# A hybrid RWKV and attention layer on one core: side work in steps of one weight unit, with TensorE's order kept in the chain

## The chip, the cores and the metric

The kernel runs on one core of a Trainium2 chip. The metric is the device time of one execution in microseconds (us), the median of three runs.

## What is computed

One layer of a streaming encoder over 16 meta tokens and 512 frames, width 1024, f32: a half-step feed-forward network (FFN1), the mixing (RWKV-7 heads beside sliding-window attention), a second half-step (FFN2) and a norm. Cut to what matters here:

```python
h = concat([meta, x])                                  # 528 x 1024
h = h + 0.5 * swiglu(rmsnorm(h, ffn1_norm), ...)       # 1024 -> 2816 -> 1024
z = rmsnorm(h, mix_norm) @ w_in
def step(S, inp):                                      # RWKV-7, one token after the other
    r_t, w_t, k_t, v_t, kk_t, a_t = inp
    sa = einsum('bhvk,bhk->bhv', S, -kk_t)
    S = S * w_t[:, :, None, :] + sa[..., None] * (kk_t * a_t)[:, :, None, :] + v_t[..., None] * k_t[:, :, None, :]
    return S, einsum('bhvk,bhk->bhv', S, r_t)
y_rwkv = group_norm_and_gate(scan(step, S0, ...))      # 8 heads of 64
y_attn = swa_sink_attention(q, k, v, sinks)            # chunks of 64, window 128, 8 heads on 2 kv heads
h = h + concat([y_rwkv, y_attn]) @ w_out
h = h + 0.5 * swiglu(rmsnorm(h, ffn2_norm), ...)
return rmsnorm(h, final_norm)[:, 16:]
```

## The kernel before

**The stream.** Activations lie transposed, features on partitions and time on columns, in two halves: the first has 272 columns (16 meta, 256 frames), the second 256. Weights pass as *units* of 128 x 1024: SP loads `raw` from DRAM, ScalarE (ACT) rounds it into `whi` (L122), VectorE (DVE) takes the rest into `wlo` (L125), and TensorE (PE) does 24 matmuls, 16 with `whi` (L213, L214) and 8 with `wlo` (L195, L222), into a bank `big`. `drive` (L128) runs the list of units in the order that `program` writes out. Three units are prepared ahead. A half's attention and RWKV run beside units of the other half or another stage: those of the first half beside FFN1 of the second, those of the second half beside FFN2 of the first. Both must be done before `w_out` of the half, which reads `n0a`/`n0b` (`n1a`/`n1b`). The function `end` (join) stands there.

**The work beside it.** After each unit `advance` (L165) adds the unit's cost to a balance and runs steps of two generators, `rwkv` and `attn`, as long as the balance lasts. A `yield` gives the cost of a step.
- `tinv` (L703): inverts the 32 x 32 triangular diagonal blocks of `GT`, 80 of them, one on each partition. Four DMAs bring the blocks through DRAM into `zk`, then 31 steps on DVE: a product of k x k elements (L726, `tmp`), its sum (L728, into `rn`). Behind the last step come a transposing copy (L731, T1), then writes to DRAM (`d<-rn` L734, `d<-tmp` L735) and reads back into `GT`, `zk`, `t2c`, all from ACT's queue. Two sets of 32 small matmuls (L753 with `zk`, L761 with `t2c`) fill the off-diagonal blocks.
- `chain` (L767): goes through the half's chunks (five in the first, four in the second half) in turn, since state `S` passes from one to the next. `values(n)` (L784) makes a chunk's `UV` and `BT`; then come UV·GT and AR·S (L813, L816), `Rs` (L819, L820), Rs·GT (L828), and the products for `S` and `Y` (L838 to L848). Its banks are `mx`, two of them. `group_norm` (L866) ends each chunk in three steps.
- `attention` (L884): four chunks of 64, each in two pairs of heads: scores (L910), maxima (L916 to L920), exp (L924), scale (L929), transposes (L930, L932), values (L942, L945). It uses the tile `as`, two banks wide, of which there is one.

**What sets the order.** The program is traced in the order above, but each engine's final list is made by a scheduler: it simulates the engines and puts behind one another what is ready in its simulation, by the priorities of `PRIO`. PE works its list strictly in that final order. An instruction that is traced early can so be put later than stream matmuls traced after it, unless its order is pinned.

Of the kernel before, what the change touches and what calls it, by code (L numbers as in the profile page):

```python
# [9 lines left out]
AF = mybir.ActivationFunctionType  # L10
# [24 lines left out]
WARM = 12  # L35
TIW, CHW, ATW = 1.4, 0.55, 0.9
NK = D // 128
# [29 lines left out]


class Prog:
    def __init__(self, ctx, tc, io):  # L70
        self.tc, self.nc, self.io = tc, tc.nc, io
        self.A, self.V, self.P, self.PE = tc.nc.scalar, tc.nc.vector, tc.nc.gpsimd, tc.nc.tensor
        self.uid = 0
        pool = lambda name, **k: ctx.enter_context(tc.tile_pool(name=name, bufs=1, **k))
        self.cst = pool("cst")
        self.rp = pool("res")
        self.np_ = pool("npl")
        self.wp = pool("wpl")
        self.tp = pool("tpl")
        self.sl = [pool("slab0")]  # L80
        self.big = pool("big", space=PSUM)
        self.mx = pool("mx", space=PSUM)
        self.dr = pool("drm", space=DRAM)
        self.hs, self.acc, self.res = {}, {}, {}
        self.sides = []
        self.ph = ''
        self.late = []
# [78 lines left out]
    def advance(self, cost):  # L166
        for sd in list(self.sides):
            if sd not in self.sides:
                continue
            sd[1] += cost  # L170
            while sd[1] > 0:
                self.mark(self.ph or sd[2] if sd[2] == 'rwkv' else sd[2])
                with self.tc.high_priority(PRIO.get(self.ph if sd[2] == "rwkv" else "", PRIO[sd[2]])):
                    c = next(sd[0], None)
                if c is None:
                    self.sides.remove(sd)
                    break
                sd[1] -= c
# [525 lines left out]
    def tinv(self, hf, mp, tip):  # L704
# [42 lines left out]
        self.ph = 'tizo'  # L747
        yield 6.0
        pc = [(p, c, slice((p * 4 + c - 1) * 32, (p * 4 + c) * 32)) for p in range(4) for c in range(1, 5)]
# [5 lines left out]
        for h in range(2):  # L755
            (A.copy, V.tensor_copy)[h](out=Z[hr[h]], in_=bz[hr[h]])
        yield 2.0
        bo = self.mbank()
# [3 lines left out]
        for h in range(2):  # L762
            (A.copy, V.tensor_copy)[h](out=GT[hr[h], 4 * h:4 * h + 4, 1:5, 32:64],
                                       in_=bo[hr[h]].rearrange("p (h s t) -> p h s t", h=4, s=4))
        yield 2.0

    def chain(self, hf, st, mo, cp):  # L767
# [5 lines left out]
        def step():  # L773

            for n_ in list(norms):
                if next(n_, None) is None:
                    norms.remove(n_)
# [4 lines left out]
        def values(n):  # L782


            slot, tok, C = chunks[n]
            UV, BT = t(cp, [128, 2, 4, 64], "UV", bufs=2), t(cp, [128, 2, 4, 64], "BT", bufs=2)
            vr = (slice(64, 64 + C), slice(0, C))
            bs = [self.mbank() for h in range(2)]
            for p in range(4):
                for h, b in enumerate(bs):  # L790
                    PE.matmul(b[vr[h], cols(p)], st["vT", p][hs[h], tok:tok + C], self.cent[hs[h], hs[h]],  # L791
                              start=True, stop=True)
            for p in range(4):
                for r in range(2):
                    for h, b in enumerate(bs):
                        PE.matmul(b[hs[r], cols(p, 256)], self.BK[p][hs[h], slot, hs[r ^ h]], self.ident[hs[h], hs[h]],  # L796
                                  start=True, stop=True)
            for h, b in enumerate(bs):
                A.copy(out=UV[vr[h], h], in_=b[vr[h], 0:256].rearrange("p (j c) -> p j c", j=4))
                A.copy(out=BT[:, h], in_=b[:, 256:512].rearrange("p (j c) -> p j c", j=4))  # L800
            pre[n] = (UV, BT)

        values(0)
        yield CHW
        hp = [(p, h) for p in range(4) for h in range(2)]
        for n, (slot, tok, C) in enumerate(chunks):
# [5 lines left out]
            for p, h in hp:  # L812
                PE.matmul(X[ur[h], cols(p)], gt(vr, h, p, 0), UV[vr[h], h, p], start=True, stop=True)  # L813
            if slot:
                for p, h in hp:
                    PE.matmul(Z[hs[h], cols(p)], self.AR[p][hs[h], slot, 0:64], S[hs[h], p], start=True, stop=True)  # L816
# [7 lines left out]
            step()  # L824
            yield 2 * CHW
            X = self.mbank()
            for p, h in hp:
                PE.matmul(X[ur[h], cols(p)], gt(ur, h, p, 0), Rs[ur[h], cols(p)], start=True, stop=True)  # L828
            for h in range(2):
                (A.copy, V.tensor_copy)[h](out=UV[ur[h], h], in_=X[ur[h], 0:256].rearrange("p (j c) -> p j c", j=4))  # L830
            step()
            yield CHW
            if n + 1 < len(chunks):
                values(n + 1)
            yield CHW
            X, Z = self.mbank(), self.mbank()
# [16 lines left out]
            if slot:  # L853
# [3 lines left out]
                norms.append(self.group_norm(st, mo, cp, Y, slice(64 * slot - 64, 64 * slot)))  # L857
            step()
            yield 2 * CHW
        self.ph = 'gn'  # L860
        while norms:
            step()
            yield 2.0

# [20 lines left out]
    def attention(self, hf, st, mo, ap_):  # L885
        A, V, P, PE, t = self.A, self.V, self.P, self.PE, self.t
        for ci in range(4):
# [16 lines left out]
            A.copy(out=VK[0:81, 0], in_=b[0:81, 0:128])  # L904
            yield ATW
            kss = (slice(0, 64), slice(64, 128))
            for mp2 in range(2):
# [4 lines left out]
                for kv in range(2):  # L912
# [8 lines left out]
                    rows.append((s, m))  # L921
                yield ATW
                for s, m in rows:
                    A.activation(s[:, 0:W], s[:, 0:W], AF.Exp, bias=m[:, 2:3], accum_out=m[:, 3:4])  # L924
                yield ATW
                b, bo = self.banks()
                for kv, (s, m) in enumerate(rows):
                    V.reciprocal(m[:, 3:4], m[:, 3:4])
                    A.activation(s[:, 0:W], s[:, 0:W], AF.Copy, scale=m[:, 3:4])  # L929
                    PE.transpose(b[0:81, 256 * kv:256 * kv + 128], s[:, 0:81], self.ident)  # L930
                    if nw > 1:
                        PE.transpose(b[0:W - 81, 256 * kv + 128:256 * kv + 256], s[:, 81:W], self.ident)  # L932
                yield ATW
                pTs = []
# [8 lines left out]
                if nw > 1:  # L943
                    for kv, ks in enumerate(kss):
                        PE.matmul(bo[ks, 0:128], VK[0:W - 81, 1, ks], pTs[kv][0:W - 81, 1], start=False, stop=True)  # L945
                yield ATW
                ms, ts = slice(2 * mp2, 2 * mp2 + 2), slice(64 * ci, 64 * ci + 64)
# [3 lines left out]
                V.tensor_tensor(out=ml, in0=ov, in1=mh.bitcast(F32), op=ALU.subtract)  # L951
                yield ATW


def program(tc, io, out):
    with ExitStack() as ctx:
# [32 lines left out]
        def popen(name, like=None):  # L989
            c = tc.tile_pool(name=name, bufs=1)  # L990
            pools[name] = (c, c.__enter__())
            return pools[name][1]
# [17 lines left out]
        def mixing(hf):  # L1010
# [8 lines left out]
            def rwkv():  # L1019
                yield from pr.tinv(hf, pools["mix"][1], popen("ti"))  # L1020
                pclose("ti")
                cp = popen("ch")
                yield from pr.chain(hf, st, mo, cp)
                pclose("ch")

            def begin():
# [45 lines left out]
        k = 10  # L1072
# [131 lines left out]
```

## Time and profile before

| | |
|---|---|
| median of 3 runs | 1154.0 us (1153.95 to 1160.99) |
| the profiled execution | 1158.89 us |
| its span on the core | 1156.7 us |
| TensorE's mean granted clock | 0.971 |
| PE busy | 1114.7 us, 96% |
| DVE busy, ACT busy | 826.4 us (71%), 673.0 us (58%) |

In the profile, L12 is line 12 of the kernel; "idle before" is the time in which the engine did nothing ahead of an instruction, and the name behind the arrow is what ended it. A PE row's duration holds the depth of the array; its pitch is the distance of the starts. The granted clock 1.00 is 2.4 GHz. The trace's times count from the start of the span.

### The profile page before, as it was taken

Reading aid. Unit: us, or ns where it says so; the run is one execution under the profiler, and the core shown is the slowest. Engines: PE = TensorE matmul, PEld = TensorE weight load, DVE = VectorE, ACT = ScalarE, POOL = GpSimd, SP = SyncE. Lnnn points to the kernel's source line nnn. Section 1 sums busy time; section 2 is a strip of 40 time slices with the busy share of each in tenths; the row PEclk is TensorE's granted clock in tenths of the full one; section 3 lists DMA queues with packets and bytes.
Section 4 is the critical chain, followed back from the end, with each engine's and each line's share of the span. In section 5 each row is a group of like instructions: output and inputs, shape, how many; then the busy total and the mean of one; then the engine's idle time right before and its main releaser. Section 6 shows DMA issues by size and latency. Waiting matters only on the chain.

```text
span 1156.7 us, 23838 instructions
## 1 busy us (share of the span) xinstructions
PE 1114.7 (96%) x9621; PEld 1043.9 (90%) x9621; DVE 826.4 (71%) x1533; ACT 673.0 (58%) x1162; POOL 36.4 (3%) x91
## 2 busy tenths in 40 slices
PE   8999999999999998999899999997999899999996
PEld 7999999998999997899899898997889898888885
DVE  7866566776778993356888777995356677777666
ACT  7544444686757645565567685574456366545453
POOL 0000000021000000000002000000000000000000
PEclk8999999999999998899899999998899899999999
DMA  7565655544446554223355445556224356676661
GB/s 270 172 182 185 187 177 179 166 142 151 129 137 182 163 176 131 81 93 112 92 182 167 138 134 169 165 152 163 90 76 122 111 154 216 201 205 194 186 186 66
DMA packets 68721, 178.81 MB, mean 155 GB/s; under 512 B 21620, under 2 KB 26868, under 8 KB 68612
## 3 DMA queue, kind: packets, MB, share of 16 engines
q1 hardware_dynamic: 52384, 173.70, 49.1%
q10 hardware_dynamic: 16228, 3.61, 1.5%
q8 instruction: 75, 1.23, 0.4%
q14 instruction: 34, 0.28, 0.1%
HBM read 173.54 MB, written 3.74 MB: 153 GB/s over the span
## 4 chain that ended last, share of the span: by engine, by line
PE 76%; DVE 13%; DMA 4%; ACT 4%; issue 3%; ACTq 1%; SPq 0%; DVEq 0%
PE big L214 16%; PE big L213 16%; PE big L195 12%; PE big L201 10%; PE big L203 5%; DVE wlo L125 4%; PE big L222 4%; DVE tmp L726 3%; DVE rn L728 2%; PE mx L796 1%; ACT whi L122 1%; PE mx L791 1%; DMA d<-GT 1%; DMA res<-xT_in 1%; DMA d<-rn 1%
## 5 line engine op out<-in xcount | busy, mean ns | idle before, releaser
L122 ACT CAST whi<-raw 128x1024 fp32r<-128x1024 f32 (+1 forms) x321 | 334.8, 1045 | 279.0 <-PE big L214 146.8
L125 DVE TENSOR_TENSOR wlo<-raw,whi 128x1024 fp32r<-128x1024 f32 x320 | 389.7, 1219 | 119.0 <-ACT whi L122 96.2
L214 PE MATMUL big<-h,whi 128*128 128x256 f32 (+1 forms) x528 | 135.2, 289 | 0.0
L213 PE MATMUL big<-h,whi 128*128 128x256 f32 (+1 forms) x528 | 132.0, 288 | 0.0
L213 PE MATMUL big<-n0a,whi 128*128 128x272 f32 (+1 forms) x464 | 123.8, 296 | 8.2 <-ACT n0a L881 3.2
L214 PE MATMUL big<-n0a,whi 128*128 128x272 f32 (+1 forms) x464 | 123.1, 293 | 0.6 <-DVE n0a L342 0.6
L213 PE MATMUL big<-n0b,whi 128*128 128x272 f32 (+1 forms) x464 | 120.3, 290 | 0.4 <-ACT n0b L341 0.3
L214 PE MATMUL big<-n0b,whi 128*128 128x272 f32 (+1 forms) x464 | 119.7, 288 | 0.4 <-DVE n0b L342 0.4
L214 PEld LDWEIGHTS big<-h,whi 128*128 128x128 f32 x528 | 100.6, 191 | 1.5 <-issue 0.9
L213 PEld LDWEIGHTS big<-h,whi 128*128 128x128 f32 x528 | 99.7, 191 | 0.6 <-issue 0.3
L213 PEld LDWEIGHTS big<-n0a,whi 128*128 128x128 f32 x464 | 89.6, 194 | 10.6 <-ACT n0a L881 3.4
L214 PEld LDWEIGHTS big<-n0a,whi 128*128 128x128 f32 x464 | 90.0, 194 | 2.1 <-DVE n0a L342 1.0
L213 PEld LDWEIGHTS big<-n0b,whi 128*128 128x128 f32 x464 | 87.9, 190 | 2.0 <-ACT n0b L341 1.1
L214 PEld LDWEIGHTS big<-n0b,whi 128*128 128x128 f32 x464 | 87.8, 190 | 1.6 <-DVE n0b L342 0.7
L213 PE MATMUL big<-n1a,whi 128*128 128x256 f32 x288 | 76.9, 297 | 8.3 <-ACT n1a L881 4.2
L222 PE MATMUL big<-h,wlo 128*128 128x256 f32 (+1 forms) x528 | 81.3, 289 | 0.0
L195 PE MATMUL big<-n0b,wlo 128*128 128x272 f32 (+1 forms) x464 | 77.4, 288 | 0.0
L195 PE MATMUL big<-n0a,wlo 128*128 128x272 f32 (+1 forms) x464 | 76.4, 286 | 0.0
L214 PE MATMUL big<-n1a,whi 128*128 128x256 f32 x288 | 76.2, 293 | 0.0
L214 PE MATMUL big<-n1b,whi 128*128 128x256 f32 x288 | 76.1, 294 | 0.0
L213 PE MATMUL big<-n1b,whi 128*128 128x256 f32 x288 | 75.7, 292 | 0.0
L222 PEld LDWEIGHTS big<-h,wlo 128*128 128x128 f32 x528 | 71.5, 192 | 1.1 <-issue 0.6
(313 smaller groups left out, 2264.2 us busy)
## 6 DMA issues: line engine op xcount, KB each, us to landing
raw<-w_in SPq DMA_DIRECT2D x319, 512.0 KB, 3.8
outT<-o SPq DMA_DIRECT2D x8, 256.0 KB, 2.6
res<-xT_in SPq DMA_DIRECT2D x2, 544.0 KB, 4.3
res<-xT_in SPq DMA_DIRECT2D x2, 512.0 KB, 9.1
d<-GT ACTq DMA_DIRECT2D x8, 80.0 KB, 3.6
zk<-d ACTq DMA_DIRECT2D x2, 320.0 KB, 4.0
d<-rn ACTq DMA_DIRECT2D x2, 320.0 KB, 3.7
GT<-d ACTq DMA_DIRECT2D x8, 80.0 KB, 4.5
```

The source lines that it names most:

```text
L122: self.A.copy(out=hi[:, a:a + n], in_=raw[:, a:a + n])
L125: self.V.tensor_tensor(out=lo[:, 0:nk], in0=raw[:, 0:nk], in1=hi[:, 0:nk].bitcast(F32), op=ALU.subtract)
L195: self.PE.matmul(o, lo[:, k], x(k)[:, 0], start=False, stop=(k == ks[-1]))
L201: self.PE.matmul(o, hi[:, i], x(k).rearrange("p a t -> p (a t)"), start=(k == first), stop=False)
L203: self.PE.matmul(o[:, 0:256], lo[:, i], x(k)[:, 0], start=False, stop=(k == last))
L213: self.PE.matmul(o, w, x[:, 0], start=first, stop=False)
L214: self.PE.matmul(o, w, x[:, 1], start=False, stop=False)
L222: self.PE.matmul(o, lo[:, i], x(k)[:, 0], start=False, stop=(k == nk - 1))
L726: V.tensor_tensor(out=m, in0=NT[:n2, 0:k, k].unsqueeze(1).broadcast_to([n2, k, k]), in1=TI[:n2, 0:k, 0:k], op=ALU.mult)
L728: V.tensor_reduce(out=TI[:n2, 0:k, k], in_=m, op=ALU.add, axis=mybir.AxisListType.X)
L791: PE.matmul(b[vr[h], cols(p)], st["vT", p][hs[h], tok:tok + C], self.cent[hs[h], hs[h]], start=True, stop=True)
L796: PE.matmul(b[hs[r], cols(p, 256)], self.BK[p][hs[h], slot, hs[r ^ h]], self.ident[hs[h], hs[h]], start=True, stop=True)
```

## The change

1. Steps have a new end, `UNIT_END`: it sets the balance to zero and leaves the loop, so that the next step comes after one whole stream unit. All steps of attention, chain and group norm, and those of `tinv` behind the last DVE step, end so. The 31 DVE steps keep their costs.
2. PE is wrapped in `Pinned`. While `on` is set, that is from the first step of the chain to its last, each matmul or transpose that is traced, of the stream and of the attention too, is kept behind the PE instruction traced before it.
3. `values` takes the two-bank tile `as` in place of two banks `mx`.
4. In the chain, AR·S alternates with UV·GT, the norms' steps move to the beginning of the next step, and the next chunk's values follow in the step of Rs·GT. In the attention, exp, reciprocal and scale move to the scores' step, and two unit ends stand ahead of the transposes.

```diff
-TIW, CHW, ATW = 1.4, 0.55, 0.9
+TIW = 1.4
+UNIT_END = -1.0
...
+class Pinned:
+    def __init__(self, tc, pe):
+        self.tc, self.pe, self.on = tc, pe, False
+    def matmul(self, *a, **k):
+        return self.pin(self.pe.matmul(*a, **k))
+    def transpose(self, *a, **k):
+        return self.pin(self.pe.transpose(*a, **k))
+    def pin(self, ins):
+        if self.on:
+            self.tc.keep_in_program_order(ins)
+        return ins
...
-        self.A, self.V, self.P, self.PE = tc.nc.scalar, tc.nc.vector, tc.nc.gpsimd, tc.nc.tensor
+        self.A, self.V, self.P, self.PE = tc.nc.scalar, tc.nc.vector, tc.nc.gpsimd, Pinned(tc, tc.nc.tensor)
...
                 if c is None:
                     self.sides.remove(sd)
                     break
+                if c == UNIT_END:
+                    sd[1] = 0.0
+                    break
                 sd[1] -= c
...
         self.ph = 'tizo'
-        yield 6.0
+        for _ in range(4):
+            yield UNIT_END
...
-        yield 2.0
+        yield UNIT_END
...
-            bs = [self.mbank() for h in range(2)]
+            bs = self.banks()
...
         values(0)
-        yield CHW
+        yield UNIT_END
...
             for p, h in hp:
                 PE.matmul(X[ur[h], cols(p)], gt(vr, h, p, 0), UV[vr[h], h, p], start=True, stop=True)
-            if slot:
-                for p, h in hp:
+                if slot:
                     PE.matmul(Z[hs[h], cols(p)], self.AR[p][hs[h], slot, 0:64], S[hs[h], p], start=True, stop=True)
...
             step()
-            yield 2 * CHW
+            yield UNIT_END
+            step()
             X = self.mbank()
...
-            step()
-            yield CHW
             if n + 1 < len(chunks):
                 values(n + 1)
-            yield CHW
+            yield UNIT_END
+            step()
             X, Z = self.mbank(), self.mbank()
...
-            step()
-            yield 2 * CHW
+            yield UNIT_END
         self.ph = 'gn'
         while norms:
             step()
-            yield 2.0
+            yield UNIT_END
...
-                yield ATW
                 for s, m in rows:
                     A.activation(s[:, 0:W], s[:, 0:W], AF.Exp, bias=m[:, 2:3], accum_out=m[:, 3:4])
-                yield ATW
+                for s, m in rows:
+                    V.reciprocal(m[:, 3:4], m[:, 3:4])
+                    A.activation(s[:, 0:W], s[:, 0:W], AF.Copy, scale=m[:, 3:4])
+                yield UNIT_END
+                yield UNIT_END
                 b, bo = self.banks()
                 for kv, (s, m) in enumerate(rows):
-                    V.reciprocal(m[:, 3:4], m[:, 3:4])
-                    A.activation(s[:, 0:W], s[:, 0:W], AF.Copy, scale=m[:, 3:4])
                     PE.transpose(b[0:81, 256 * kv:256 * kv + 128], s[:, 0:81], self.ident)
...
-                yield ATW
+                yield UNIT_END
...
                 cp = popen("ch")
+                pr.PE.on = True
                 yield from pr.chain(hf, st, mo, cp)
                 pclose("ch")
+                pr.PE.on = False
```

**TensorE's order.** Up to the stream's matmul number 2569 (second mixing: 4731) both kernels have the same order on PE. Changed kernel, PE, behind the attention's first chunks of the first mixing (`as` from `ident,BK`: the end of values(0); `big`: a stream unit; `zk,GT` and `t2c,Z`: the matmuls behind the inverse; `UV,GT`, `Rs,GT`: chain; all PE rows have the wrapper's line):

```order
L78 MATMUL as_4654<-ident,BK_1799 64x64 x4
L78 MATMUL big_4691<-n1a_1094,whi_4464 128x256 x8
L78 MATMUL big_4691<-n1b_1095,whi_4464 128x256 x8
L78 MATMUL big_4691<-n1a_1094,wlo_4465 128x256 x4
L78 MATMUL big_4691<-n1b_1095,wlo_4465 128x256 x4
L78 MATMUL mx_4494<-zk_4328,GT 32x32 x32
L78 MATMUL mx_4572<-t2c_4329,Z_4527 32x32 x32
L78 MATMUL mx_4722<-UV_4652,GT 16x64 x8
L78 MATMUL as_4734<-KT,Q_3650 128x145 x2
L78 MATMUL big_4759<-n1a_1094,whi_4536 128x256 x8
L78 MATMUL big_4759<-n1b_1095,whi_4536 128x256 x8
L78 MATMUL big_4759<-n1a_1094,wlo_4537 128x256 x4
```

Between matmul 2569 and `zk,GT` the changed kernel has one stream unit, here as four rows, besides attention steps and values(0). From then on a step of the chain and 24 matmuls of the stream alternate, up to the last `gsq` product at stream matmul 2977. In the second mixing the same holds: one unit between matmul 4731 and `zk,GT`, the last `gsq` product at 5067.

Kernel before, PE, at the same matmuls `zk,GT` (L753), with the stream's `whi` and an attention product (L942) about them:

```order
L214 MATMUL big_6231<-n1b_1095,whi_6127 128x256
L213 MATMUL big_6231<-n1b_1095,whi_6127 128x256
L753 MATMUL mx_4586<-zk_4463,GT 32x32 x18
L942 MATMUL as_4356<-pT_4399,VK_4300 64x128
L753 MATMUL mx_4586<-zk_4463,GT 32x32
L942 MATMUL as_4356<-pT_4402,VK_4300 64x128
```

Before, `zk,GT` begins among stream matmuls 3150 (second mixing: 5276), 581 and 545 matmuls further on, and the last `gsq` product stands at 3657 (5691), where the stretch of the stream ends and `w_out` begins. The chain's instructions lie among the stream in 53 and 47 pieces before, and in 24 and 24 now.

**VectorE's order.** Changed kernel, DVE, the last four steps of the first inverse (`tmp`, `rn`: the inverse; `wlo`: a unit's rest; `silu`, `h_697`: FFN1):

```order
L749 TENSOR_TENSOR tmp_3665<-zk_3660,rn_3662 80x784
L751 TENSOR_REDUCE rn_3662<-tmp_3665 80x28
L145 TENSOR_TENSOR wlo_4687<-raw_4685,whi_4686 128x1024
L419 TENSOR_TENSOR silu_4717<-big_4691,silu_4717 128x256
L749 TENSOR_TENSOR tmp_3665<-zk_3660,rn_3662 80x841
L421 TENSOR_TENSOR h_697_4716<-silu_4717,h_697_4716 128x256
L751 TENSOR_REDUCE rn_3662<-tmp_3665 80x29
L749 TENSOR_TENSOR tmp_3665<-zk_3660,rn_3662 80x900
L751 TENSOR_REDUCE rn_3662<-tmp_3665 80x30
L749 TENSOR_TENSOR tmp_3665<-zk_3660,rn_3662 80x961
L751 TENSOR_REDUCE rn_3662<-tmp_3665 80x31
L754 COPY tmp_4322<-rn_3662 80x1024
```

Kernel before, DVE, its last two steps (L726, L728), `res`: the stream's sums (L441):

```order
L726 TENSOR_TENSOR tmp_3665<-zk_3660,rn_3662 80x900
L951 TENSOR_TENSOR n0b_3618<-as_4240,n0b_3618 128x2x64
L441 SCALAR_TENSOR_TENSOR res_150<-big_5972,res_150 128x256
L125 TENSOR_TENSOR wlo_5968<-raw_5966,whi_5967 128x1024
L728 TENSOR_REDUCE rn_3662<-tmp_3665 80x30
L441 SCALAR_TENSOR_TENSOR res_150<-big_6004,res_150 128x256
L125 TENSOR_TENSOR wlo_6000<-raw_5998,whi_5999 128x1024
L726 TENSOR_TENSOR tmp_3665<-zk_3660,rn_3662 80x961
L441 SCALAR_TENSOR_TENSOR res_150<-big_6036,res_150 128x256
L125 TENSOR_TENSOR wlo_6032<-raw_6030,whi_6031 128x1024
L728 TENSOR_REDUCE rn_3662<-tmp_3665 80x31
L916 ISA s_4344,m_4345<-as_4341,tabm 128x17
```

From the twelfth step on the changed kernel has one `wlo` among the inverse's rows; in the kernel before there are twenty.

## Rows read from the trace of the kernel before

**Rows 1.** Windows: busy us and count per engine, granted clock, DMA share, GB/s.
```profile
361.90:441.20 79.30, 76.09 (x632) 73.26 (x630) 71.03 (x142) 43.74 (x84) 0.00 (x0) 1.00 0.57 168
441.20:560.40 119.20, 119.16 (x1512) 106.66 (x1513) 65.44 (x137) 70.85 (x142) 0.00 (x0) 0.91 0.34 103
560.40:575.50 15.10, 11.29 (x64) 10.39 (x63) 12.88 (x25) 7.11 (x15) 0.10 (x1) 0.77 0.16 39
723.50:796.00 72.50, 71.61 (x602) 68.74 (x600) 66.95 (x126) 42.09 (x76) 6.43 (x8) 1.00 0.58 171
796.00:902.90 106.90, 100.68 (x1317) 90.18 (x1317) 56.23 (x122) 59.07 (x125) 0.48 (x2) 0.92 0.34 98
902.90:913.60 10.70, 6.54 (x34) 6.51 (x34) 5.01 (x7) 2.65 (x4) 0.00 (x0) 0.68 0.00 1
```

**Rows 2.** Timeline of PE: start, us, line, operation, count [idle before].
```profile
361.90 0.28 PE L213 MATMUL big<-n1a,whi 128*128 128x256 f32 x1
...
428.52 0.28 PE L213 MATMUL big<-n1a,whi 128*128 128x256 f32 x1
...
431.39 0.28 PE L213 MATMUL big<-n1a,whi 128*128 128x256 f32 x1
...
454.52 1.07 PE L761 MATMUL mx<-t2c,Z 32*32 32x32 f32 x56
```

**Rows 3.** Timeline of DVE: where the inverses stand and end.
```profile
363.24 0.41 DVE L726 TENSOR_TENSOR tmp<-zk,rn 80x144 f32<-80x144 f32 x1
...
723.64 0.57 DVE L726 TENSOR_TENSOR tmp<-zk,rn 80x225 f32<-80x225 f32 x1
...
784.41 1.18 DVE L728 TENSOR_REDUCE rn<-tmp 80x31 f32<-80x961 f32 x1
```

**Rows 4.** DVE by line from 363.2 to 428 us: busy, mean ns of one.
```profile
L125 DVE TENSOR_TENSOR wlo<-raw,whi 128x1024 fp32r<-128x1024 f32 x20 | 24.2, 1211 | 0.0
...
L726 DVE TENSOR_TENSOR tmp<-zk,rn 80x144 f32<-80x144 f32 (+19 forms) x20 | 21.3, 1067 | 0.1
...
L728 DVE TENSOR_REDUCE rn<-tmp 80x11 f32<-80x121 f32 (+20 forms) x21 | 13.5, 642 | 0.1
...
L918 DVE CUSTOM_DVE_ANT_0 s<-as,tabw 128x128 f32<-128x128 f32 (+1 forms) x6 | 1.6, 265 | 0.0
...
L920 DVE TENSOR_SCALAR m<-m 128x1 f32<-128x1 f32 x6 | 1.1, 201 | 0.0
```

**Rows 5.** DVE by line from 723.6 to 785.6 us.
```profile
L726 DVE TENSOR_TENSOR tmp<-zk,rn 80x225 f32<-80x225 f32 (+16 forms) x17 | 19.9, 1172 | 0.2
...
L728 DVE TENSOR_REDUCE rn<-tmp 80x14 f32<-80x196 f32 (+17 forms) x18 | 12.7, 707 | 0.2
```

**Rows 6.** Timelines: first write behind the inverse (ACT's queue), first matmul on its return (PE).
```profile
785.62 0.32 ACTq L734 DMA_DIRECT2D d<-rn  x1
...
797.01 0.24 PE L753 MATMUL mx<-zk,GT 32*32 32x32 f32 x2 [1.20 <-DMA zk<-d]
```

**Rows 7.** The page, DMA issues: operation, queue, count, KB each, median us to landing.
```profile
d<-rn ACTq DMA_DIRECT2D x2, 320.0 KB, 3.7
...
GT<-d ACTq DMA_DIRECT2D x8, 80.0 KB, 4.5
```

**Rows 8.** ACT by line from 441.2 to 560.4 us: busy, mean ns | idle before.
```profile
L122 ACT CAST whi<-raw 128x1024 fp32r<-128x1024 f32 x23 | 24.1, 1047 | 15.0 <-PE big L214 11.2 <-issue 2.4 <-ACT BT L800 0.9
...
L924 ACT ACT_TABLE_LOAD x3 | 3.8, 1283 | 0.1
...
L819 ACT COPY Rs<-mx 128x256 f32<-128x256 f32 x4 | 1.5, 371 | 1.6 <-PE mx L813 1.6
```

**Rows 9.** Timeline of PE about a return from a chain step to the stream.
```profile
532.79 0.39 PE L214 MATMUL big<-h,whi 128*128 128x256 f32 x1
...
533.02 0.28 PE L213 MATMUL big<-h,whi 128*128 128x256 f32 x1
...
533.14 0.28 PE L214 MATMUL big<-h,whi 128*128 128x256 f32 x1
```

More of the change, by code (lines that the diff above doesn't have):

```diff
@@ L862, in chain @@
             step()
-            yield 2.0
+            yield UNIT_END
     def group_norm(self, st, mo, cp, Y, ts):
@@ L921, in attention @@
                     rows.append((s, m))
-                yield ATW
                 for s, m in rows:
                     A.activation(s[:, 0:W], s[:, 0:W], AF.Exp, bias=m[:, 2:3], accum_out=m[:, 3:4])
-                yield ATW
+                for s, m in rows:
+                    V.reciprocal(m[:, 3:4], m[:, 3:4])
+                    A.activation(s[:, 0:W], s[:, 0:W], AF.Copy, scale=m[:, 3:4])
+                yield UNIT_END
+                yield UNIT_END
                 b, bo = self.banks()
                 for kv, (s, m) in enumerate(rows):
-                    V.reciprocal(m[:, 3:4], m[:, 3:4])
-                    A.activation(s[:, 0:W], s[:, 0:W], AF.Copy, scale=m[:, 3:4])
                     PE.transpose(b[0:81, 256 * kv:256 * kv + 128], s[:, 0:81], self.ident)
@@ L932, in attention @@
                         PE.transpose(b[0:W - 81, 256 * kv + 128:256 * kv + 256], s[:, 81:W], self.ident)
-                yield ATW
+                yield UNIT_END
                 pTs = []
@@ L945, in attention @@
                         PE.matmul(bo[ks, 0:128], VK[0:W - 81, 1, ks], pTs[kv][0:W - 81, 1], start=False, stop=True)
-                yield ATW
+                yield UNIT_END
                 ms, ts = slice(2 * mp2, 2 * mp2 + 2), slice(64 * ci, 64 * ci + 64)
@@ L951, in attention @@
                 V.tensor_tensor(out=ml, in0=ov, in1=mh.bitcast(F32), op=ALU.subtract)
-                yield ATW
+                yield UNIT_END
 def program(tc, io, out):
```

## The prediction

> **What bounds the kernel now.** The table ahead names the bound: TensorE is busy for 96% of the span, and most of that is the stream. So the question to each view is where TensorE stands still or runs slowly, and which of its instructions the change makes wait. I read first the windows over the two mixings, then the DVE timeline of the inverses, then the orders of both kernels.
>
> The windows [rows 1] cut each mixing in three. While the inverse runs on DVE (361.9 to 441.2 us, 723.5 to 796.0), TensorE works nearly all the time: idle for 79.30 − 76.09 = 3.2 and 72.50 − 71.61 = 0.9 us, at a granted clock of 1.00 (2.4 GHz). In the stretch of the chain it is idle for 0.0 and 6.2, at clocks of 0.91 and 0.92. In the short stretch behind, about the beginning of `w_out`, it is idle for 3.8 and 4.2, at 0.77 and 0.68. The reader is to see that the inverse costs TensorE nothing today, because 581 and 545 matmuls of the stream lie beside it (a unit of 24 has a pitch of 431.39 − 428.52 = 2.87 us [rows 2]), and that all that a better placed chain could give back lies in the second and third windows.
>
> Then DVE. At 363.24 the first inverse begins step 12 (144 elements), at 723.64 the second begins step 15 (225 elements) [rows 3]. From there the steps themselves take 21.3 + 13.5 = 34.8 us [rows 4] and 19.9 + 12.7 = 32.6 [rows 5]; before, they are spread to twice that, since twenty `wlo` (24.2 us [rows 4]) and other rows of the stream lie between. The steps depend on one another, and with nothing between them they still take these 34.8 and 32.6 us.
>
> **The change part by part.**
>
> *The inverse comes to stand ahead of TensorE.* In the changed order `zk,GT`, which needs the inverse back from DRAM, stands one unit behind stream matmul 2569. Before, TensorE passes that matmul at 361.9 [rows 2], when 20 steps of the inverse are still to come. Chain matmuls are pinned behind one another and all later stream matmuls behind them, and they need `GT` with the inverse in it. So nothing can go ahead on TensorE, and queued behind it is the whole stream: its banks do not come free, ACT and DVE prepare three units and stop. First mixing: from 363.2 DVE does 34.8 of steps, attention rows of two pairs of heads (L918 and L920 take 2.7 for six tiles [rows 4]; with the rows not shown some 3 for four, an estimate), two `wlo` (2.4), `silu` and `h` (0.8), and waits for two exp with their table loads (1.28 each [rows 8], so 2.6): 43.6, which ends at 406.8. Then the way through DRAM. In the second mixing it lasts from the first write's issue at 785.62 to the first `zk,GT` at 797.01, for which TensorE waited 1.2 us [rows 6]: 11.4. Behind it the two sets of 32 matmuls, the copies of Z and GT, four copies of values(0), which ACT holds back until then, and UV·GT: a set is estimated at 1.2 (56 matmuls in 1.07 [rows 2]) and a copy of a bank at 0.37 (L819 [rows 8]), so 2.4 + 0.7 + 0.7 + 1.5 + some 1.7 for the matmuls and handovers, 7.0 together. The stream goes on at 425.2, 63.3 after 361.9. In this time TensorE does one unit (2.9), both sets (2.4), values, scores, transposes and products (some 5): 10 of use, 53 lost. Second mixing in the same way: 32.6 + 3 + 2.4 + 0.8 + 2.6 = 41.4 from 723.6, then 11.4 and 7.0, which ends at 783.4; less 723.5 and 10: 50 lost. Sum of both: +103. Bounds: with the steps alone, one table load and 5 us behind the way, 1.3 (361.9 to 363.2) + 34.8 + 1.3 + 11.4 + 5 − 10 = 44, in the second mixing 0.1 + 32.6 + 1.3 + 11.4 + 5 − 10 = 40, or 84; and with 5 more of waits in each, 113.
>
> Of the way through DRAM: the trace's own medians are 3.7 us to landing for a write of the inverse and 4.5 for a read back [rows 7], two after one another 8.2 of the 11.4. The Trainium skill, page "DMA: Bandwidth & Descriptors", section "Latency and other measured facts", speaks of a fixed cost of about 2 us for a DMA. By that the two would take about 4, the sum would be 2 × 4.2 = 8 lower, an estimate; the trace disagrees, and its durations stand in the sum.
>
> *Behind a standstill the clock is low.* After the waits of 3 to 4 us at `w_out` the windows show 0.77 over 15.1 us and 0.68 over 10.7: 3.5 and 3.4 us lost [rows 1]. The stall is longer, so I take such a loss once for each mixing: +7 (0 to 14).
>
> *What comes back.* The chain ends 680 and 624 matmuls earlier than now (2977 against 3657, 5067 against 5691), so `w_out` finds its operands ready. The idle time of the six windows goes, 3.2 + 0.0 + 3.8 + 0.9 + 6.2 + 4.2 = 18.3; the low clock at `w_out` goes, 3.5 + 3.4 = 6.9; and of the low clock in the chain's stretches, 0.09 × 119.2 + 0.08 × 106.9 = 19.3, I take half, 9.6, since the same small matmuls remain, in half as many places. Together −35 (−25 without that half, −44 with all).
>
> *Fewer changes between chain and stream.* The chain lies in 48 pieces for 100, 52 fewer. At the return from one, the first stream matmul's distance to the next is 533.02 − 532.79 = 0.23, where 533.14 − 533.02 = 0.12 is the rule [rows 9], so 0.1 for each end: 52 × 2 × 0.1 = −10 (0 to −10).
>
> *The pinned steps.* Each of some 31 steps of the chain finds one unit, 2.87 us, between itself and the step before, and TensorE cannot pass it. In that time its copy and its sum (0.37 and about 0.4) have to be made, with one weight copy of ACT (1.05 [rows 8]) and one `wlo` (1.21 [rows 4]) ahead of them: 3.0 and handovers, about as much as there is. I take 0.4 for each, +12; the bounds are 0, since TensorE's rows of the chain now show no idle time in the first window, and a whole weight copy with the step's own copy, 1.4, or +44.
>
> *The rest.* values in the `as` tile, the alternated matmuls, the moved norms and the attention's exp in an earlier step leave the count of instructions as it is. They cost nothing beside the unit between steps; without that cover they are within the 1.4 above. The `as` tile is shared with the attention, and a wait for it would show as one more of these.
>
> **Sum.** 103 + 7 − 35 − 10 + 12 = +77. The profiled execution took 1158.89, which gives 1236; its time stands 4.9 above the median of the runs shown, and so the forecast is 1231 us, 6.7% above 1154.0.
>
> **The rivals.**
> - *The chain pays off (faster).* If the inverse comes back about when TensorE gets to `zk,GT`, no stall and all that can come back: −44 − 10 + 12 = −42, 1112 us. For it speaks that the chain's late end is a real loss today. It needs a stall of less than 21 us for each mixing, since 42 is all there is; against it speak the steps' 34.8 and 32.6 us [rows 4, 5], on one engine in a row of dependences, and the order, in which one unit stands for them. Chance 0.02.
> - *Short stall.* Inverse at its bare length (84), clock costs of 7, all of the 44 and 10 come back, the pinned steps wait for nothing: +37, 1191 us. For it: DVE has no other rows to do but these; against it: attention rows stand between them and have waits for ACT. Chance 0.13.
> - *Each step of the chain waits.* ACT and DVE work their own lists in order, and if a weight copy stands ahead of every chain copy, each of 31 steps costs 1.4. With the long stall of 113, and no clock coming back in the chain: 113 + 7 − 25 − 10 + 44 = +129, 1278 us. Chance 0.16.
> - *The change does nothing that can be measured.* For this the stall would have to be 42 by chance; a measurement of this kernel tells about 1% from no change. Chance 0.01.
>
> **How the numbers follow.** The forecast has 0.68. Its own spread, from the bounds of stall (84 to 113) and of the steps, is 1205 to 1260. The range of 8 in 10 takes in the short stall and the lower part of the waiting chain: 1188 to 1275. Faster has the first rival's 0.02, no change 0.01, slower 0.97.
>
> **What would show it.** Right: in the changed trace TensorE has one idle time of some 30 us or more in each mixing, ended by the DMA of `zk` or by the copies behind it; ACT and DVE have no weight copies to do in it; DVE does the last steps of the inverse one right behind another; the granted clock is low after it and 1.00 up to `w_out`; and the `n0a` and `n1a` waits at `w_out` are gone. Each chain matmul behind a unit shows an idle time of some tenths. Wrong: stream matmuls between 365 and 420 us as now; or idle times of more than a microsecond ahead of most of the chain's steps; or a chain that still ends at `w_out`.

## The result, and the profile after

The changed kernel takes 1190.96 us (median of 4 runs, 1188.21 to 1191.02) beside 1153.97 for the kernel before: a ratio of 1.030, 95% interval 1.026 to 1.035. It is slower, as forecast, but by 37 us and not by 77.

The page of the changed kernel: busy time, and the clock in 40 slices.

```profile
PE 1082.3 (91%) x9621; PEld 1016.5 (85%) x9621; DVE 829.9 (70%) x1533; ACT 674.1 (57%) x1163; POOL 33.0 (3%) x91
...
PEclk8999999999996589999999999659999999999999
```

TensorE has the same 9621 matmuls as before and is busy for 32 us less, though more of that time is at the low clock. Two holes in the clock are new. The windows of the changed kernel (PE, PEld, DVE, ACT, POOL, then granted clock, DMA share, GB/s): three stretches of the first standstill; then two about `w_out`, which begins at 582.8 and answers to the third of [rows 1].

```profile
362.00:382.00 20.00, 6.84 (x36) 3.15 (x36) 18.30 (x57) 7.10 (x25) 0.00 (x0) 0.64 0.18 53
382.00:410.40 28.40, 6.82 (x73) 6.30 (x68) 21.52 (x20) 1.46 (x2) 0.00 (x0) 0.56 0.24 54
410.40:420.40 10.00, 6.44 (x148) 5.26 (x148) 1.38 (x2) 2.96 (x8) 0.00 (x0) 0.50 0.10 17
591.90:607.00 15.10, 15.10 (x128) 15.10 (x127) 13.72 (x27) 9.76 (x17) 0.00 (x0) 1.00 0.61 182
560.00:591.90 31.90, 31.90 (x270) 31.85 (x270) 22.09 (x33) 17.33 (x24) 0.00 (x0) 1.00 0.58 181
```

From 362 to 420.4 TensorE does 20 us of work, at half the clock for much of it, and ACT 11.5. From 560 to 607, the beginning of `w_out` among it, TensorE never waits and the clock is full. TensorE's timeline shows what the longest idle times in the first standstill wait for:

```profile
368.01 0.94 PE L81 MATMUL as<-ident,s 128*81 128x128 f32 x2 [4.93 <-ACT s L948]
...
377.08 1.54 PE L81 MATMUL as<-ident,s 128*81 128x128 f32 x4 [3.68 <-ACT s L948]
...
410.37 0.31 PE L78 MATMUL mx<-zk,GT 32*32 32x32 f32 x2 [21.58 <-DMA zk<-d]
411.84 1.91 PE L78 MATMUL mx<-zk,GT 32*32 32x32 f32 x62 [1.16 <-DMA zk<-d]
...
418.75 1.03 PE L78 MATMUL mx<-UV,GT 16*16 16x64 f32 x14 [0.26 <-ACT UV L823]
```

The second mixing has the same: 17.16 us ahead of `zk,GT` at 785.99. The shorter waits are for the attention's exp and scale (`s`). On DVE the inverse now runs on almost alone (DVE by line from 363 to 410 us, which answers to [rows 4], and its end):

```profile
L749 DVE TENSOR_TENSOR tmp<-zk,rn 80x144 f32<-80x144 f32 (+19 forms) x20 | 20.0, 998 | 0.5
L751 DVE TENSOR_REDUCE rn<-tmp 80x11 f32<-80x121 f32 (+20 forms) x21 | 13.6, 646 | 0.5
L145 DVE TENSOR_TENSOR wlo<-raw,whi 128x1024 fp32r<-128x1024 f32 x2 | 2.4, 1210 | 0.0
```

```profile
402.97 1.03 DVE L754 COPY tmp<-rn 80x1024 f32<-80x1024 f32 x1
```

**How the runs are read.** The stream's matmuls are numbered in order. The delay of each stream matmul against the kernel before grows to 83 us at matmul 3000 and is down to 15 at 3720, behind the first `w_out` units; in the second mixing it goes from 17 to 95 and back to 33. So a mixing is measured between stream matmuls that all kernels share: 2530 to 3720 and 4690 to 5760. Each such stretch is split into TensorE's idle time, half of its busy time at the granted clock 0.5 (what the low clock costs), and the rest, busy time less that half: the time TensorE's work would take at full clock. Both mixings together, in us, worked out from the rows of PE and the clock of each trace:

| kernel | median | idle | low clock costs | work at full clock |
|---|---|---|---|---|
| before | 1154.0 | 18.4 | 23.0 | 379.4 |
| changed | 1191.0 | 82.5 | 26.8 | 342.3 |
| no pin (x1) | 1140.4 | 29.2 | 13.6 | 356.0 |
| 27 unit ends (x2) | 1144.8 | 40.3 | 22.6 | 343.4 |
| 24 unit ends (x3) | 1148.5 | 46.2 | 23.0 | 342.1 |
| 27 unit ends, `mx` (y1) | 1167.3 | 47.0 | 33.8 | 346.3 |
| no pin, `mx` (y3) | 1140.5 | 17.3 | 7.4 | 370.3 |
| before with `as` (y4) | 1150.3 | 35.2 | 15.4 | 362.6 |
| attention later, pin early (z1) | 1134.8 | 36.3 | 9.3 | 345.8 |
| one unit later (z2) | 1145.7 | 41.4 | 20.0 | 345.7 |
| z1 with half after half (z3) | 1140.6 | 35.1 | 9.6 | 354.1 |

From before to changed: idle +64, clock +4, work −37, sum +31; the span grew by 32.5. The columns come from one execution of each kernel, and that of the kernel before took 4.9 us more than its median, that of y3 3.3 less; runs of the kernel before differ with the granted clock (1150.98 us at 0.980, 1158.13 at 0.971), so the column of the low clock is the least certain.

### The profile page after: what moved, and what is told of

Same layout as the page of the kernel before. It is cut to its first block, busy times and chain, and to the rows that moved or that the text cites. A ratio compares the mean times of both kernels' runs of the same rounds, so it can differ in the third digit from the quotient of the medians.

```text
span 1189.2 us, 23831 instructions
## 1 busy us (share of the span) xinstructions
PE 1082.3 (91%) x9621; PEld 1016.5 (85%) x9621; DVE 829.9 (70%) x1533; ACT 674.1 (57%) x1163; POOL 33.0 (3%) x91
## 4 chain that ended last, share of the span: by engine, by line
PE 76%; DVE 12%; ACT 5%; DMA 3%; issue 2%; ACTq 1%; DVEq 0%; SPq 0%
PE big L78 70%; PE mx L78 4%; DVE tmp L749 3%; DVE wlo L145 2%; DVE rn L751 2%; PE as L78 2%; ACT whi L142 2%; DMA zk<-d 1%; DMA d<-GT 1%; DVE grs L897 1%; ACT L896 1%; PE as L81 1%; DMA d<-rn 1%; DMA raw<-w_in 0%; ACT s L945 0%
## 5 line engine op out<-in xcount | busy, mean ns | idle before, releaser
L78 PE MATMUL big<-h,whi 128*128 128x256 f32 (+2 forms) x1232 | 192.4, 303 | 3.4 <-DVE res L464 1.3
L78 PE MATMUL big<-n0a,whi 128*128 128x272 f32 (+1 forms) x928 | 140.9, 292 | 4.4 <-ACT Q L631 1.5
L78 PE MATMUL big<-n0b,whi 128*128 128x272 f32 (+1 forms) x928 | 137.5, 289 | 1.0 <-ACT n0b L364 0.5
L78 PE MATMUL big<-n1a,whi 128*128 128x256 f32 (+1 forms) x752 | 135.5, 317 | 0.7 <-ACT Q L631 0.7
L78 PE MATMUL big<-n1b,whi 128*128 128x256 f32 (+1 forms) x752 | 132.6, 314 | 0.0
L78 PEld LDWEIGHTS big<-n1b,whi 128*128 128x128 f32 x752 | 110.3, 195 | 8.2 <-issue 0.2
L78 PEld LDWEIGHTS big<-n1a,whi 128*128 128x128 f32 x752 | 107.2, 195 | 8.1 <-issue 2.1
L78 PE MATMUL big<-n1b,wlo 128*128 128x256 f32 x464 | 76.2, 285 | 0.0
L78 PE MATMUL big<-n1a,wlo 128*128 128x256 f32 x464 | 75.3, 285 | 0.0
L78 PEld LDWEIGHTS big<-n1a,wlo 128*128 128x128 f32 x464 | 67.5, 193 | 3.7 <-issue 0.2
```

The lines of the kernel that those rows point to most:

```text
L78: return self.pin(self.pe.matmul(*a, **k))
```

## The experiments

**x1: the pin away.**

```diff
-                pr.PE.on = True
...
-                pr.PE.on = False
```

> The changed kernel with the pinning never switched on; everything else stays. Theory (the pin puts the inverse ahead of TensorE, and the pinned order is also what makes the small matmuls cheaper): the two standstills of 38 and 36 us idle go, the order puts the matmuls behind the inverse at stream matmul 3112 and 5241; the pitch of side matmul to side matmul goes back from 29-30 ns to about 40, so TensorE's full-clock work in the two mixings is back near 200 and 180 us; 1135 to 1155 us. Rival (unit ends, two-bank tile and alternated matmuls make the small matmuls cheaper, without the pin): the pitch stays near 30 ns, work stays near 180 and 162, 1100 to 1120 us.

Measured: 1140.39 us, ratio 0.986 (0.983 to 0.988): 1.4% faster than the kernel before, and within what the theory expected. The windows of its two mixings:

```profile
357.40:565.00 207.60, 192.38 (x2262) 180.87 (x2262) 153.47 (x309) 126.25 (x247) 0.10 (x1) 0.98 0.44 133
708.40:899.60 191.20, 177.16 (x2038) 166.67 (x2037) 136.83 (x274) 109.16 (x214) 2.63 (x10) 0.95 0.43 130
```

And of the same stretches of the changed kernel, where 235.00 − 193.76 = 41.2 is the idle time of the first:

```profile
356.90:591.90 235.00, 193.76 (x2263) 180.91 (x2262) 153.84 (x306) 122.94 (x241) 0.10 (x1) 0.88 0.40 118
734.10:950.80 216.70, 175.35 (x2038) 163.62 (x2037) 139.16 (x277) 113.19 (x220) 3.97 (x10) 0.88 0.39 116
```

The standstills are gone: the pin costs 50.6 us (idle 53, clock 13, less 14 of work that it saves). The work lies between both expectations, 356: of the 37 us saved, 23 come from the rest of the change and 14 from the pin. The pitch from one side matmul to the next is 32 ns here, 42 and 44 before, 29 and 30 in the changed kernel.

**x2, x3: more units between the inverse and the chain.**

```diff
-        for _ in range(4):
+        for _ in range(27):        # x3: 24
             yield UNIT_END
```

> The changed kernel with 27 unit ends behind the last step of the inverse in place of 4, so that the pinned chain starts when the inverse is back (first matmuls behind it at stream matmul 3120 and 5275-5280, last gsq product at 3528 and 5616, both ahead of w_out). Theory (the standstill is the only loss, the smaller TensorE work is a gain of the pinned order): idle under 15 us in the two mixings together, full-clock work again near 180 and 162 us, 1095 to 1115 us. Rival (the work fell only because the chain ran behind a standstill, with DVE and ACT free of the stream's backlog): work near 190 and 172 or idle over 25 us, 1130 to 1160 us.

> The same with 24 unit ends: the first matmuls behind the inverse stand at stream matmul 3048 and 5208, about three units (9 us) ahead of where the inverse comes back in the kernel before. Theory: a standstill of 3 to 10 us in each mixing, and 8 to 20 us more than with 27 unit ends. Rival (with the wlo rows of the stream beside it DVE ends the inverse no later than the order assumes): no difference, within 3 us.

Measured: 1144.78 (0.990, 0.988 to 0.992) and 1148.53 (0.993, 0.992 to 0.995). The work is the pinned kernel's, 343 and 342, so the saving does not need the standstill: that part of the rival falls. But 40 us of idle time stay, where the theory expected under 15, and the times are the rival's. In x3 `zk,GT` waits 12.5 us in the first mixing and not in the second, where a wait of 9.8 us takes its place (it is told at z1). In x2 little of it waits for the inverse (5.2 us for the DMA of `zk`). Its timeline about the start of the chain:

```profile
453.61 1.14 PE L81 MATMUL as<-ident,s 128*81 128x128 f32 x4 [3.36 <-ACT s L948]
455.60 1.12 PE L78 MATMUL as<-pT,VK 81*64 81x128 f32 x8 [0.85 <-ACT pT L962]
457.51 0.69 PE L81 MATMUL as<-ident,VC 128*81 128x128 f32 x2 [0.78 <-DVE n0b L974]
458.71 1.07 PE L78 MATMUL as<-KC,Q 64*128 64x209 f32 x4 [0.52 <-ACT VK L926]
462.31 0.93 PE L81 MATMUL as<-ident,s 128*81 128x128 f32 x3 [2.53 <-ACT s L948]
```

These are attention steps in a row with no stream matmul between, though each ends with a unit end: steps traced before, left behind, and then due at once. The longest waits are for exp and scale (`s`), the others for copies and sums. The three units between x3 and x2 are worth 6 us of idle time and 3.8 us of time, in the direction of the theory and less than its 8 to 20; the step from 4 units to 24 was worth 42.

**x4: the pin alone, on the kernel before.**

```diff
+                pr.PE.on = True
                 yield from pr.chain(hf, st, mo, cp)
                 pclose("ch")
+                pr.PE.on = False
```

> The kernel before with the pinning alone; costs, banks and order of the steps as before. The first matmuls behind the inverse stand at stream matmul 2520 and 4656, and the whole chain lies in 13 pieces within some 170 stream matmuls. Theory (the pin alone makes the standstill; the unit ends then hide the chain's own waits): a standstill of 45 us or more idle in each mixing, and idle time of more than 1 us ahead of most chain steps, some 30 us in each; 1230 to 1290 us. Rival (the standstill comes from the unit ends): none over 15 us, under 1170.

Measured: 1257.96 us, in one run alone. The stream stops once for 75 us in the first mixing and once for 81 in the second. In the stretches 2300 to 3720 and 4450 to 5760 (its chain begins before 2530) TensorE is idle for 59.5 and 57.9 us; the kernel before has 7.2 and 13.2 there.

```profile
324.20:627.80 303.60, 244.12 (x2546) 223.98 (x2546) 179.18 (x371) 138.91 (x268) 1.64 (x7) 0.83 0.36 108
736.40:1017.50 281.10, 223.22 (x2325) 204.19 (x2324) 165.31 (x340) 122.74 (x249) 6.97 (x17) 0.82 0.36 109
```

So the pin makes the standstill, without any unit end; behind it the chain's steps wait for some 17 and 13 us, less than the 30 expected in each. The standstill has another face than expected: `zk,GT` itself waits 1.1 us only, since a whole row of attention steps, each with its own wait (up to 6.4 us), stands ahead of it while DVE ends the inverse. With the rest of the change, the unit ends among it, the pinned kernel is 67 us faster.

**y1: 27 unit ends and the values in `mx`; y2: the pin on from the start of the side work.**

```diff
-            bs = self.banks()
+            bs = [self.mbank() for h in range(2)]      # y1
...
                 pr.side(rwkv(), "rwkv")
+                pr.PE.on = True                            # y2, with 29 unit ends
```

> 27 unit ends behind the inverse, pin on, and the values of a chunk in two one-bank tiles mx again. With 27 unit ends and the two-bank tile 40 us of idle time stayed in the two mixings, most of it ahead of attention instructions that came in a row about the start of the chain. Theory (values(0) needs the tile as, so the pinned start waits for all attention steps left behind, one after the other): with mx the idle time of the two mixings falls from 40 to under 20 us and the low clock with it, 1115 to 1130 us. Rival (it is the attention's own steps, pinned behind one another, that wait, whichever tile values takes): idle still 30 us or more, 1138 to 1152 us.

> The pin on from the start of the side work of a mixing (attention and inverse too), 29 unit ends behind the inverse (first matmuls behind it at stream matmul 3120 and 5280). Theory (attention steps, kept one unit apart from the first, pile up nowhere, so the start of the chain finds nothing to wait for): idle under 20 us in the two mixings together, full-clock work near 180 and 162, 1105 to 1125 us. Rival (the attention's steps wait for DVE, which has the inverse's rows ahead of them, and now hold up the stream): idle over 40 us, 1145 to 1175 us.

Measured: 1167.34 (1.011, 1.008 to 1.013) and 1185.44 (1.027, 1.024 to 1.029). Both missed. In y1 the attention's waits stayed (13.6 us ahead of `ident,s`, 15.1 in x2) and one came to them: `cent,vT` waits for a bank that `UV`'s copy on DVE has to leave, 13.0 us in 7 waits. In y2 the mixings' own stretches became the shortest of all (189 and 175 us, with 6.7 and 9.5 idle), and 41 and 37 us were lost before them: the pin flushed the projections' last products, which used to stand about stream matmul 2414 and now stood at 2016 to 2026, behind DVE's preparation.

```profile
301.44 0.90 PE L78 MATMUL mx<-AR,BK 64*64 64x128 f32 x3 [3.91 <-DVE BK L693]
308.63 0.60 PE L78 MATMUL as<-La,wah 128*128 128x272 f32 x1 [1.12 <-DVE bv L621]
312.41 0.66 PE L78 MATMUL as<-AR,BK 64*64 64x128 f32 x2 [2.66 <-DVE BK L693]
```

It is the changed kernel's mistake once more, one phase earlier.

**y3: no pin and values in `mx`; y4: the kernel before with values in `as`.** The line of `values` as in y1, without the pin; and turned over, in the kernel before.

> No pin (as in the run without pinning, 1140 us), and values in two one-bank tiles mx again: unit ends, alternated matmuls and moved steps are left of the change. Theory (with both banks free at once a chunk's values are issued in the order of the loop, which alternates halves of the array; with one bank after the other they are not): the values' matmuls (cent,vT and ident,BK) cost 11 to 12 and 9 to 10 us of TensorE time in the two mixings as in the kernel before, in place of 5.8 and 4.5, so 1148 to 1158 us. Rival (the gain is the unit ends'): within 4 us of 1140.

> The kernel before with a chunk's values in the two-bank tile as, nothing else. Theory: the values' matmuls fall from 12.2 and 9.8 us of TensorE time to about 6 and 4.5, 12 us less work; but values now wait for the attention at the tile as, and the chain's last matmuls come as late as stream matmul 3672 and 5688, so the idle time at w_out stays or grows by some us: 1140 to 1156 us. Rival (the order inside values is set by readiness, not by the tile): work as before, and the later chain makes it 1156 to 1170 us.

Measured: 1140.54 (0.989, 0.985 to 0.992) and 1150.32 (0.997, 0.995 to 0.998). TensorE by line, `values` in the first mixing, of the kernel before:

```profile
L796 PE MATMUL mx<-ident,BK 64*64 64x64 f32 x160 | 9.9, 232 | 0.0
L791 PE MATMUL mx<-cent,vT 64*64 64x64 f32 (+1 forms) x80 | 8.3, 226 | 0.0
```

The same of y3:

```profile
L78 PE MATMUL mx<-ident,BK 64*64 64x64 f32 x160 | 9.1, 233 | 0.0
L78 PE MATMUL mx<-cent,vT 64*64 64x64 f32 (+1 forms) x80 | 7.4, 232 | 3.4 <-ACT grs L896 3.2 <-DVE UV L854 0.2
```

And of x1, whose window leaves out values(0), 48 of the 240 matmuls:

```profile
L78 PE MATMUL as<-ident,BK 64*64 64x64 f32 x128 | 4.6, 225 | 0.0
L78 PE MATMUL as<-cent,vT 64*64 64x64 f32 x64 | 2.7, 224 | 0.0
```

The tile alone saves 14 us of work in y3 against x1 and 17 in y4 against before. It gives most of it back, 12 and 17 us more idle time, so that y3 is as fast as x1 (the rival's time, though the work went the theory's way) and y4 only 4 us faster than before. Why is not shown: in neither trace does a wait in the mixings end with the tile `as` coming free. In x1 the longest are for the stream's `whi` (12.3 us in 3), in y4 for `gsq` (7.5 in 2), which stands later in the stream there than before. With the pin on, the tile saves only 3 us of work (y1 against x2): what the tile and the pin save is in part the same.

**z1, z2: attention later, pin from its first step.**

```diff
 def attention
+        for _ in range(11):        # z2: 12
+            yield UNIT_END
+        PE.on = True
...
-        for _ in range(4):         # tinv; PE.on = True ahead of the chain goes
+        for _ in range(29):        # z2: 30
             yield UNIT_END
```

> The pin begins at the attention's first step, the attention begins 11 units later than in the changed kernel (when the tile as is free of the projections' work), and 29 unit ends stand behind the inverse. The projections' matmuls stand where they do in the kernel before, the first attention scores at stream matmul 2472, the first matmuls behind the inverse at 3120 and 5280. Theory (what was lost with 27 unit ends is attention steps left behind, with the pin from the start the projections' matmuls flushed early; without both the pinned order only gains): idle under 20 us in the two mixings together, full-clock work near 180 and 160 us, 1095 to 1112 us. Rival (pinned attention steps each wait for exp and for DVE, with the inverse's rows ahead): idle over 40 us, 1135 us or more.

> The same with the attention 12 units later and 30 unit ends (first matmuls behind the inverse at stream matmul 3144 and 5304, one unit later). Theory: within 4 us of the run with 11 and 29, since the inverse is back at both. Rival (the inverse is back only at about 3150, so each unit of 2.87 us counts in both mixings): 4 to 8 us less than that run.

Measured: z1 1134.81 us, ratio 0.984 (0.981 to 0.986), the fastest run of this study; z2 1145.65 (0.993, 0.991 to 0.996). The backlog was part of x2's loss: z1 is 10 us faster, with 4 us less idle time, 13 less at the low clock, 2 more of work and 4 to 5 more outside the two stretches. But 36 us of idle time stay, between the two expectations: in the stretches 16.9 us are waits for the tile `as` (in 5) and 11.4 for exp and scale (in 7). The longest of them (TensorE, then ACT) is not the attention's own:

```profile
436.89 1.07 PE L78 MATMUL as<-KT,Q 64*128 64x209 f32 x4 [9.30 <-ACT VK L929]
```

```profile
430.39 2.73 ACTq L763 DMA_DIRECT2D GT<-d  x4
...
435.46 1.04 ACT L142 CAST whi<-raw 128x1024 fp32r<-128x1024 f32 x1 [8.98 <-DMA zk<-d]
436.42 0.26 ACT L928 COPY VK<-as 128x128 f32<-128x128 f32 x1
436.57 0.26 ACT L929 COPY VK<-as 81x128 f32<-81x128 f32 x1
```

The copy to `VK`, which frees `as`, stands in ACT's list behind the DMA issues of the inverse, and ACT stands idle for 9 us until the reads have gone out behind the writes. x3 has the same in its second mixing, with 9.8 us ahead of `KC,Q`. No run gave these DMAs to another queue.

z2 missed both ways. One unit later costs 11 us: 5 more idle and 11 more at the low clock in the two stretches, less 5 outside them. Its waits for exp and scale are longer (19.0 us in 10 for 11.4 in 7); why, and why the clock falls for so much longer, stays open.

**z3: the turn of the halves.** In `values` of z1, the loop over the head half moved outside (`for h` ahead of `for p`); the same matmuls in the same pieces.

> The run with 11 and 29, and in values the loops turned over: all matmuls of one head half, then all of the other, in place of halves in turn. Same instructions, same pieces. Theory (a small matmul can overlap the one before it only in another part of the array, so the turn of the halves is what makes them cheap): the pitch of cent,vT goes from 25 to 50-60 ns and that of ident,BK up too, values' TensorE time from about 5 and 4 us to 10 and 8; 6 to 12 us slower. Rival (the small matmuls are cheap because nothing of the stream or of another step stands between them): no difference, within 3 us.

Measured: 1140.60 (0.989, 0.987 to 0.992), 5.8 us more than z1, work +8.3: the theory's direction, a little under its 6 to 12. TensorE by line in the first mixing, of z1:

```profile
L78 PE MATMUL as<-ident,BK 64*64 64x64 f32 x160 | 4.1, 222 | 0.0
L78 PE MATMUL as<-cent,vT 64*64 64x64 f32 (+1 forms) x80 | 3.3, 223 | 0.0
```

And of z3:

```profile
L78 PE MATMUL as<-ident,BK 64*64 64x64 f32 x160 | 7.7, 224 | 0.0
L78 PE MATMUL as<-cent,vT 64*64 64x64 f32 (+1 forms) x80 | 4.7, 223 | 0.0
```

One matmul lasts 222 to 224 ns either way; what changes is how many are under way at once. In one chunk of z1, and then of z3:

```profile
475.52 0.51 PE L78 MATMUL as<-cent,vT 64*64 64x64 f32 x10
```

```profile
476.19 0.79 PE L78 MATMUL as<-cent,vT 64*64 64x64 f32 x13
```

In z1 ten `cent,vT` start within 0.29 us, 32 ns apart; in z3 thirteen within 0.57, 48 apart. From one matmul of `values` to the next it is 19 ns in z1 and 39 in z3 on average over both mixings, 45 in the kernel before and 18 in the changed one (from the starts in each trace, the low clock taken out). So matmuls of one half still overlap (48 ns apart, 224 long), only less. The Trainium skill, page "TensorEngine Tiling (Array Packing)", section "Key Properties", states that tiles work independently, and that different ones can load weights and multiply in parallel. These rows agree. Half and bank change together in this loop, and which of the two it takes was not tried.

## Why the prediction was right in direction and wrong in size

- *Standstill, +103: right in kind, 12 too dear.* It stands where the text said, in both mixings, with the DMA of `zk` at its end and hardly any stream work on ACT. The first lasted from 361.9 to 420.5 us, where 425.2 was worked out. DVE's steps took 33.6 for 34.8, its waits less. The way through DRAM took 7.4 us to the first `zk,GT` (402.97 to 410.37) and 8.9 to the bulk of them, not 11.4; what stands behind it took 10.1, at half clock, not 7.0. The text counted as lost what is not work at full clock. By that the first standstill lost 47.7 us (38.3 idle, 9.4 at the low clock) and the second 43.0 (34.1 and 8.9, from 741.0 to 795.9): 91 for 103.
- *Clock outside the standstills, −10 in all (+7 behind them, −6.9 at `w_out`, −9.6 in the chain): right in direction, too small.* The low clock costs the changed kernel 26.8 us, 18.3 of them in the standstills; the 8.5 left stand for 23.0 before: −14.5. The low clock at `w_out` went, as said.
- *Idle time coming back, −18, and pinned steps, +12: near.* At `w_out` nothing waits; outside the standstills the changed kernel is idle for 10 us in both mixings, the kernel before for 18: −8 for −6.
- *Fewer changes between chain and stream, −10: right.* Steps from stream to side and back are 102 before and 52 now in these stretches; with the stream's matmuls taken at their own pitch that is 12 us.
- *"The rest ... leave the count of instructions as it is. They cost nothing beside the unit between steps": this step failed.* It counted the small matmuls and took their time as given. Some 1930 of them stood at 42 and 44 ns from one another, some 1980 now at 29 and 30: 82 us became 58. *The pinned steps* had priced waits alone, not this. Taken away in this turn, y3, x1 and the changed kernel part it: the whole work fell by 9 us with unit ends, alternated matmuls and moved steps, by 14 with the two-bank tile and by 14 with the pin (in another turn the tile saves 17 without the rest, y4, and 3 under the pin, y1). 13 of the 25 us lie in `values` (21 to 8), and z3 shows how an order can cost them; that the scheduler had in fact put matmuls of one half behind one another, as their one bank came free, is inferred from the pitch, since no row names the half. The other 12 lie in the chain's other products, `UV,BT` first (10 to 5.5), and how the pin makes them cheaper was not tried. With this term, −25, the sum would have been 1206. Of the other 15 us to the measured time most is the standstill's 12.
- *The rivals.* The time of "short stall" (1191) came out by luck. Its stall of 84 and clock cost of 7 are the 91 measured; but it has 44 us of idle time and clock come back, where 23 did, and 10 less work, where it was 37: two errors that nearly cancel. "The chain pays off" fails by the standstill alone: without it (x1, z1) it is what happens, 14 to 19 us faster and not 42. "Each step of the chain waits" asks for 44 us where 10 are idle; its sum, 1154 + 129, is 1283 and not 1278.

## What to carry to other kernels

Before an engine's order is pinned, ask for each pinned instruction what stands in the trace behind it and whether its inputs are there at that place: the pin turned work that the scheduler had hidden (34 us of an inverse on DVE) into a standstill of the whole stream, and the attempts to move the pin or its start (x2, x3, y2) found the next step left behind. Count small matmuls not by number but by their pitch, and look at which part of the array follows which; an order, or a tile that frees two banks at once, can be worth as much as a wait. Ask also whose list the DMA issues stand in, and what stands behind them. Where a change has several parts, run each alone: here the pin hid a gain of 14 us in the others.

## What was not expected of the hardware

A DMA landing is shorter in the changed kernel: its page has 2.5 us for a read of the inverse and 2.7 for a write, before 4.5 and 3.7 [rows 7].

```profile
d<-rn ACTq DMA_DIRECT2D x2, 320.0 KB, 2.7
GT<-d ACTq DMA_DIRECT2D x8, 80.0 KB, 2.5
```

In these runs it goes with what else the DMA engines move, not with TensorE's stream. These are the windows about the reads in the changed kernel, the kernel before, y2 and x3 (the last two numbers are DMA share and GB/s):

```profile
405.70:409.50 3.80, 0.00 (x0) 0.00 (x0) 0.00 (x0) 0.00 (x0) 0.00 (x0) 0.50 0.67 106
431.60:439.00 7.40, 6.25 (x52) 5.99 (x50) 1.61 (x4) 1.85 (x6) 0.00 (x0) 1.00 0.77 200
399.70:403.50 3.80, 3.80 (x30) 3.32 (x30) 0.42 (x1) 0.00 (x0) 0.00 (x0) 0.88 0.66 104
787.90:795.00 7.10, 0.00 (x0) 0.00 (x0) 0.31 (x1) 0.00 (x0) 0.52 (x1) 0.58 0.85 207
```

In y2 TensorE works all the time and the reads land in 2.1 to 2.4 us; in x3 it stands still and they take 5.9 to 6.6, beside weights that are still being fetched. In all runs the reads land in 2.0 to 2.9 us where 104 to 131 GB/s are moved, and in 2.5 to 6.7 where it is 184 to 252. The prediction weighed a page of the Trainium skill against the longer durations; the same section of "DMA: Bandwidth & Descriptors" in the Trainium skill adds that the fixed cost falls with the load on HBM. These rows agree with that. The two landings of the changed kernel, 5.2 us together, lie between the 4 that the prediction worked out from that page, an estimate, and the 8.2 of its sum.
